# Issuing the pieces of turned attention weights, queries and keys from GpSimd, and taking each head norm's factor in one power

## The chip, the cores and the metric

The kernel runs on one core of one Trainium2 chip. The metric is the device time of one execution in microseconds (us). "PE" or TensorE multiplies matrices, "DVE" or VectorE and "ACT" or ScalarE work element by element, "POOL" or GpSimd does small element work and issues DMAs, and "SP" or SyncE issues DMAs only. A DMA issued by SP and one issued by GpSimd appear in the profile on different queues (q1 and q0).

## The reference, cut to what matters

The model is a trunk of two layers over 256 tokens of width 2048, with 256 memory tokens. Each layer has a token mixer of 12 heads of 128 beside 4 cross-attention heads into the memory, one output projection, and a squared-ReLU MLP of width 8192. Layer 0 has mixer A (neighbourhood attention), layer 1 has mixer B: grouped-query attention with 12 query heads and 4 key/value heads. Only mixer B normalises its heads:

```python
n = rms_norm(h, attn_norm[i])
z = n @ b_w_in[j]
q, k, v, qm = jnp.split(z, [MIX_WIDTH, MIX_WIDTH + KV_WIDTH, MIX_WIDTH + 2 * KV_WIDTH], axis=-1)
q = axial_rope(rms_norm(split_heads(q, N_MIX_HEADS), b_q_norm[j]))
k = axial_rope(rms_norm(split_heads(k, N_KV_HEADS), b_k_norm[j]))
...
def rms_norm(x, g):
    y = xf * lax.rsqrt(jnp.mean(xf * xf, axis=-1, keepdims=True) + EPS)
```

EPS is 1e-6. Every attention is softmax(q k^T) v in float32.

## The kernel before, in words

All weights are float32 and are loaded once, by SP, in chunks of 128 x 2048 (1 MB). Each half of a chunk is split by ScalarE and VectorE into a high and a low part (`hi`, `lo`, line 331 and the line before it), and TensorE makes each product as three: high by high, low by high, high by low. The chunks are worked off in halves called grains; a list of grains is the program's order, and a "tick" passes with each grain. A half is split three grains ahead of its products (`ahead=(8, 5, 3)`), a chunk's buffer is one of three (`raw`), and the split halves have four (`hi`, `lo`). Work that follows from a block of products (`later(n, ...)`) is put into the order n ticks on. The program is written in this order, and a planner that simulates a timeline places each engine's instructions in its own queue; an engine works its queue off in order.

Mixer A and the cross-attention of both layers, and most heads of mixer B, need the attention weights with keys along the partitions. They are not transposed by TensorE, but "turned": `attend` makes the scores and the softmax; `turned` lets VectorE transpose blocks of 32 x 32 within partitions (line 417), and `moved` carries the blocks between partitions by DMA: four "pieces" (line 382), one for each group of 32 partitions, go to a buffer in DRAM, 64 KB each, and one "return" (line 383), 256 KB, brings it back. The return is issued by GpSimd and waits for the pieces' landing. A few ticks later `attend2_turned` splits what came back into `pT`, and `attend3` makes the products `av` (lines 444 to 446). There are 26 such turns: 4 heads of cross-attention and 12 of mixer A in layer 0, 4 of cross-attention and 6 of mixer B in layer 1.

`heads_turned` does the same with a block of four heads of queries or keys in layer 1: two tiles of 128 tokens each, for the cross-attention queries (`b_qm_done`), the keys (`b_k_done`) and the first block of queries (`b_q_done`, block 0). Blocks 1 and 2 of the queries are transposed by TensorE (`heads_T`, tile `pt_h`). `turned_rows` uses `moved` as well, for the residual stream around the MLPs.

`normed_heads` takes a block of products in PSUM, unnormalised, and for each of two tiles: ScalarE squares each of four heads with the row's factor `rstd` as scale and sums the squares (line 1199); VectorE makes mean + EPS (`b_r_v`, line 337); GpSimd raises it to -0.5 (`b_r_r`, line 339) and multiplies by `rstd` (line 1202); ScalarE scales the heads by the result (line 1205); VectorE applies the rotary tables (lines 1207 to 1215), which gives `b_o`. It runs for the keys and for the three blocks of queries: 8 tiles.

Of the kernel before, what the change touches and what calls it, by code (L numbers as in the profile page):

```python
# [10 lines left out]
F32 = mybir.dt.float32  # L11
# [3 lines left out]
ALU = mybir.AluOpType  # L15
AX = mybir.AxisListType

P = 128
D = 2048
SEQ = 256  # L20
NT = SEQ // P
KT = D // P
DFF = 8192
HD = 128
# [7 lines left out]
EPS = 1e-6  # L32
# [59 lines left out]
def encoder_kernel(ctx: ExitStack, tc: tile.TileContext, t: dict, out: bass.AP):  # L92
    nc = tc.nc
# [3 lines left out]
    def opened(name, side="left", space=None, bufs=1):  # L97
        kw = {"space": space} if space else {}
        manager = tc.tile_pool(name=name, bufs=bufs, side=side, reuse_waits="tile", **kw)
        pools[name] = manager, manager.__enter__()  # L100
        return pools[name][1]

    def closed(*names):
        for name in names:
            pools.pop(name)[0].__exit__(None, None, None)

    const = opened("const")
    keep = opened("keep")
    small = opened("small", bufs=3)
# [10 lines left out]
    def open_ring():  # L120
        at.ring = opened("ring")
        at.cat = opened("cat")
# [32 lines left out]
    mhalf = const.tile([P, 8], F32, name="mhalf")  # L155
# [63 lines left out]
    def later(n, fn, *args):  # L219
        pending.append((state["tick"] + n, fn, args))  # L220
# [107 lines left out]
    def split(dst_hi, dst_lo, src):  # L328

        first = nc.scalar.activation(dst_hi, src, AF.Copy)  # L330
        return first, nc.vector.tensor_tensor(dst_lo, src, dst_hi.bitcast(F32), op=ALU.subtract)  # L331

    def rstd_of(ss, n, name):

        w = ss.shape[-1]
        v = small.tile([P, w], F32, tag="rs_v", name=f"{name}_v")
        nc.vector.tensor_scalar(v, ss, 1.0 / n, EPS, op0=ALU.mult, op1=ALU.add)
        r = small.tile([P, w], F32, tag="rs_r", name=f"{name}_r")
        nc.gpsimd.tensor_tensor(r, v, mhalf[:, :w], op=ALU.pow)
        return r  # L340
# [32 lines left out]
        return s  # L373


    def moved(dst, src):

        f = dst.shape[-1]
        x = dram.tile([P, 4, f], F32, tag=f"turn{f}", bufs=4, name="turn")
        to = x.rearrange("(b r) a f -> a r b f", r=32)  # L380
        for a in range(4):
            nc.sync.dma_start(to[a], src[32 * a : 32 * a + 32])
        nc.gpsimd.dma_start(dst, x)

    def scores(name):
        return at.work.tile([P, NT, SEQ], F32, tag="sc", bufs=at.scores, name=name)
# [27 lines left out]
    def turned(sc):  # L414

        x = scores("sc_t").rearrange("p a b -> p (a b)")
        nc.vector.transpose(x.rearrange("p (b k s j) -> p s k b j", b=4, k=2, s=2),
                            sc.rearrange("p s (k b r) -> p s k b r", k=2, b=4))
        back = sc.rearrange("p a b -> p (a b)").rearrange("p (a f) -> p a f", a=4)
        moved(back, x.rearrange("p (b f) -> p b f", b=4))  # L420
        return back

    def attend2_turned(back, o=0):
# [64 lines left out]
    def wide(name, at=0):  # L488
        room = keep.tile([P, KT * 512 + P], F32R, tag="wide", name=name)
        return room[:, at // 4 : at // 4 + KT * 512].rearrange("p (a b) -> p a b", b=512)  # L490
# [186 lines left out]
    def sum_squares(which, i, nb):  # L677
        sq = at.side.tile([P, 512], BF16, tag="junk", bufs=1, name="sq")
        nc.scalar.activation(sq, h[:, i, nb * 512 : (nb + 1) * 512], AF.Square,
                             accum_out=ssq[which][:, i, nb : nb + 1])  # L680

    def mean_square(which, n, name):

        s = small.tile([P, NT], F32, tag="ss0", name="ss_t")
        nc.vector.tensor_reduce(s, ssq[which][:, :, :n], axis=AX.X, op=ALU.add)
        v = keep.tile([P, NT], F32, tag=name, name=name)
        nc.vector.tensor_scalar(v, s, 1.0 / (n * 512), EPS, op0=ALU.mult, op1=ALU.add)
        return v

    def past(fn, ins=None):  # L690

        a, v = ins or box["ready"]
        with tc.issue_after(a.ins), tc.issue_after(v.ins):
            fn()

    def turned_rows(src, room, back):

        nc.vector.transpose(room.rearrange("p (b k i j) -> p i k b j", b=4, k=4, i=2),
                            src.rearrange("p i (k b r) -> p i k b r", k=4, b=4))
        back = back.rearrange("p (a f) -> p a f", a=4)  # L700
        moved(back, room.rearrange("p (b f) -> p b f", b=4))
        return back
# [259 lines left out]
    def add_scaled(hs, src, factor):  # L962
        nc.vector.scalar_tensor_tensor(hs, src, factor, hs, op0=ALU.mult, op1=ALU.add)
# [122 lines left out]
    def down_done(layer, nb):  # L1086
        def f(w):
            for i in range(NT):
                add_scaled(h[:, i, nb * 512 : (nb + 1) * 512], w.ps[i], box["inv"][:, i : i + 1])
            for i in range(NT):  # L1090
                sum_squares(2 * layer + 1, i, nb)
            if layer == 1:
                later(1, times_gf, nb)
                return
            if nb == 0:
                box["nT"] = wide("nT1", 480)
            if nb == 3:
                closed("mlp")
                open_ring()
            later(1, turned_input, nb)  # L1100
            if nb == 3:

                def norm():
                    box["rstd"] = keep.tile([P, NT], F32, name="rstd1")
                    box["mean"] = mean_square(1, 4, "mean")
                    nc.gpsimd.tensor_tensor(box["rstd"], box["mean"], mhalf[:, :NT], op=ALU.pow)
                later(2, norm)
        return f

# [63 lines left out]
    def heads_turned(src, dst):  # L1173

        backs = []
        for i in range(NT):
            room = scores("h_t").rearrange("p a b -> p (a b)")
            nc.vector.transpose(room.rearrange("p (b k j) -> p k b j", b=4, k=4),
                                src[i].rearrange("p (k b r) -> p k b r", k=4, b=4))
            back = src[i].rearrange("p (a f) -> p a f", a=4)  # L1180
            moved(back, room.rearrange("p (b f) -> p b f", b=4))
            backs.append(back)

        def heads_landed():
            for i in range(NT):
                hi, lo = (dst[:, :, x * SEQ + i * P : x * SEQ + (i + 1) * P].rearrange("p k (a j) -> p k a j", a=4)
                          for x in range(2))
                split(hi, lo, backs[i].rearrange("p a (k j) -> p k a j", k=4))

        later(5, lambda: past(heads_landed, box["splits"][-1]))  # L1190

    def normed_heads(w):
        cg, sg = box["rope"]
        outs = []
        for i in range(NT):
            y2 = at.work.tile([P, 4, HD], F32, tag="b_y2", name="b_y2")
            ss = small.tile([P, 4], F32, tag="b_ss", name="b_ss")
            for j in range(4):
                nc.scalar.activation(y2[:, j, :], w.ps[i][:, j * HD : (j + 1) * HD], AF.Square,
                                     scale=box["rstd"][:, i : i + 1], accum_out=ss[:, j : j + 1])  # L1200
            r = rstd_of(ss, HD, "b_r")
            nc.gpsimd.tensor_scalar(r, r, box["rstd"][:, i : i + 1], None, op0=ALU.mult)
            y = at.work.tile([P, 4, HD], F32, tag="b_y", name="b_y")
            for j in range(4):
                nc.scalar.activation(y[:, j, :], w.ps[i][:, j * HD : (j + 1) * HD], AF.Copy, scale=r[:, j : j + 1])
            o = at.work.tile([P, 4, HD], F32, tag="b_o", bufs=3, name="b_o")
            nc.vector.tensor_tensor(o, y, cg[:, i, None, :].to_broadcast([P, 4, HD]), op=ALU.mult)
            yv = y.rearrange("p h (a b c) -> p h a b c", a=2, b=2)
            y2v = y2.rearrange("p h (a b c) -> p h a b c", a=2, b=2)
            sv = sg[:, i, :].rearrange("p (a b c) -> p a b c", a=2, b=2)  # L1210
            for a in range(2):
                for b in range(2):
                    nc.vector.tensor_tensor(y2v[:, :, a, b, :], yv[:, :, a, 1 - b, :],
                                            sv[:, None, a, b, :].to_broadcast([P, 4, 32]), op=ALU.mult)
            nc.vector.tensor_tensor(o, o, y2, op=ALU.add)
            outs.append(o.rearrange("p a b -> p (a b)"))
        return outs

    def b_k_done(w):
        outs = normed_heads(w)  # L1220
        box["kT"] = keys("kT1")
        later(1, heads_turned, outs, box["kT"])
        later(3, rope_tables, "q", C_QN, SCALE)
# [190 lines left out]
```

## Time and profile before

| what | value |
|---|---|
| median of three runs | 2014.71 us (2011.62 to 2015.72) |
| the profiled execution | 2011.52 us |
| its span, first to last instruction | 2009.4 us |
| TensorE busy | 1997.4 us, 99% |
| VectorE busy | 1691.8 us, 84% |
| ScalarE busy | 1245.8 us, 62% |
| GpSimd busy | 142.7 us, 7% |
| DMA | 461.13 MB, mean 229 GB/s |

The stages lie so in the span: memory products from 0 to some 100 us, mixer A to some 330, output projection and MLP of layer 0 to some 1050, input products of mixer B to some 1220, its last heads beside the first products with w_o about 1220 to 1290, then the output projection and the MLP of layer 1 to the end. In the rows of time the first two columns are the start and the duration in us; the name before "<-" is the tile written, those behind it the tiles read; "L" is the line of the kernel; the bracket is the engine's idle time before the instruction and what ended it. "x4" merges four rows. In a view of one tile the three durations are least, median and greatest in ns, followed by the first and last start.

### The profile page before, as it was taken

The page shows a single profiled execution, that of the slowest core. Times are in us where ns is not written, and L with a number is a line of the kernel's source. Part 1 is how long each engine was busy: PE and PEld are TensorE (multiplying, and loading weights), DVE is VectorE, ACT ScalarE, POOL GpSimd, SP SyncE. Part 2 cuts the span into 40 slices and gives each one's busy share as a digit, 9 for nine tenths or more (in the row PEclk, how much of TensorE's full clock was granted, in tenths as well). Part 3 has the DMA queues.
Part 4 walks back from the last instruction along what each step waited for, and adds up shares of the span by engine and source line. Part 5 has one row for each costly group of instructions (what it writes and reads, how often), then busy time and mean ns, then how long its engine had stood idle before and what let it go on. Part 6 is the DMA issues. An engine that isn't in the chain of part 4 may idle for free.

```text
span 2009.4 us, 32896 instructions
## 1 busy us (share of the span) xinstructions
PE 1997.4 (99%) x12945; PEld 1807.2 (90%) x12945; DVE 1691.8 (84%) x2080; ACT 1245.8 (62%) x1650; POOL 142.7 (7%) x185
## 2 busy tenths in 40 slices
PE   9999999999999999999999999999999999999998
PEld 8999999899999999999988888889999999999997
DVE  6767767669998999999998778768989999999896
ACT  6755555557666666666655567657666666666664
POOL 0000000000000000000000112000000000000000
PEclk9999999999999999999999999999999999999999
DMA  7766666847777787787767776557777777777763
GB/s 286 300 224 217 219 222 210 329 134 236 223 232 232 233 233 235 217 244 236 216 215 262 257 260 213 216 190 239 227 231 223 235 229 234 225 239 231 235 224 115
DMA packets 121626, 461.13 MB, mean 229 GB/s; under 512 B 13824, under 2 KB 36992, under 8 KB 88320
## 3 DMA queue, kind: packets, MB, share of 16 engines
q1 hardware_dynamic: 100080, 412.90, 61.3%
q0 software_dynamic: 20816, 45.10, 10.5%
q8 instruction: 101, 1.65, 0.3%
q10 hardware_dynamic: 576, 1.05, 0.1%
q14 instruction: 53, 0.43, 0.1%
HBM read 411.80 MB, written 17.83 MB: 214 GB/s over the span
## 4 chain that ended last, share of the span: by engine, by line
PE 94%; DMA 2%; DVE 2%; issue 1%; ACT 1%; SPq 0%; POOLq 0%; POOL 0%; DVEq 0%; ACTq 0%
PE ps_u L825 12%; PE ps_u L824 12%; PE ps_u L823 12%; PE p L942 9%; PE p L941 9%; PE p L940 9%; PE ps_m L242 7%; PE ps_m L238 7%; PE ps_m L241 7%; PE ps_s L250 3%; PE ps_s L252 3%; PE ps_s L251 3%; DMA sc<-turn 1%; DVE lo L331 1%; DMA raw<-in_w_o 1%
## 5 line engine op out<-in xcount | busy, mean ns | idle before, releaser
L825 PE MATMUL ps_u<-hT,ul 128*128 128x256 f32 x2048 | 566.4, 277 | 0.0
L824 PE MATMUL ps_u<-hT,uh 128*128 128x256 f32 x2048 | 565.1, 276 | 0.0
L823 PE MATMUL ps_u<-hT,uh 128*128 128x256 f32 x2048 | 564.5, 276 | 0.0
L330 ACT ACTIVATE uh<-raw_U 128x1024 fp32r<-128x1024 f32 x278 | 294.5, 1061 | 297.8 <-PE ps_u L824 280.3
L824 PEld LDWEIGHTS ps_u<-hT,uh 128*128 128x128 f32 x2048 | 384.3, 188 | 6.6
L823 PEld LDWEIGHTS ps_u<-hT,uh 128*128 128x128 f32 x2048 | 384.2, 188 | 5.6
L825 PEld LDWEIGHTS ps_u<-hT,ul 128*128 128x128 f32 x2048 | 384.3, 188 | 0.1
L331 DVE TENSOR_TENSOR ul<-raw_U,uh 128x1024 fp32r<-128x1024 f32 x278 | 337.6, 1219 | 25.5 <-ACT uh L330 25.5
L331 DVE TENSOR_TENSOR lo<-raw,hi 128x1024 fp32r<-128x1024 f32 (+1 forms) x224 | 265.1, 1191 | 102.5 <-ACT hi L330 99.9
L330 ACT ACTIVATE hi<-raw 128x1024 fp32r<-128x1024 f32 (+1 forms) x224 | 230.4, 1038 | 166.3 <-PE ps_m L242 65.7
L330 ACT ACTIVATE th<-t 128x2048 fp32r<-128x2048 f32 x112 | 215.1, 1921 | 115.4 <-PE p L942 108.8
L331 DVE TENSOR_TENSOR tl<-t,th 128x2048 fp32r<-128x2048 f32 x112 | 256.2, 2288 | 28.1 <-ACT th L330 27.4
L331 DVE TENSOR_TENSOR bl<-b,bh 128x1536 fp32r<-128x1536 f32 x112 | 196.3, 1753 | 5.3 <-ACT bh L330 5.3
L330 ACT ACTIVATE bh<-b 128x1536 fp32r<-128x1536 f32 x112 | 166.7, 1488 | 19.4 <-PE p L942 13.2
L920 POOL DMA_DIRECT2D t<-b x112 | 96.5, 861 | 1126.0 <-DVE t L919 419.7
L942 PE MATMUL p<-th,a_s 128*128 128x512 f32 x448 | 176.3, 393 | 0.0
L941 PE MATMUL p<-tl,a_s 128*128 128x512 f32 x448 | 176.0, 393 | 0.0
L940 PE MATMUL p<-th,a_s 128*128 128x512 f32 x448 | 159.1, 390 | 0.0
L942 PE MATMUL p<-bh,a_s 128*128 128x512 f32 x336 | 131.7, 392 | 0.0
L941 PE MATMUL p<-bl,a_s 128*128 128x512 f32 x336 | 131.1, 390 | 0.0
L251 PE MATMUL ps_s<-nT,hi 128*128 128x256 f32 x448 | 124.1, 277 | 0.0
L250 PE MATMUL ps_s<-nT,hi 128*128 128x256 f32 x448 | 123.9, 277 | 0.0
(288 smaller groups left out, 3790.0 us busy)
## 6 DMA issues: line engine op xcount, KB each, us to landing
raw_U<-in_w_up SPq DMA_DIRECT2D x128, 1024.0 KB, 7.5
b<-in_w_pair SPq DMA_DIRECT2D x112, 768.0 KB, 4.9
raw<-in_w_o SPq DMA_DIRECT2D x32, 1024.0 KB, 5.6
t<-in_w_pair SPq DMA_DIRECT2D x112, 256.0 KB, 3.3
t<-b POOLq DMA_DIRECT2D x112, 256.0 KB, 7.3
raw<-in_w_b SPq DMA_DIRECT2D x21, 1024.0 KB, 5.9
raw<-in_w_av SPq DMA_DIRECT2D x12, 1024.0 KB, 5.1
raw<-in_w_aq SPq DMA_DIRECT2D x12, 1024.0 KB, 5.1
```

What stands on the lines that cost most here:

```text
L238: first = nc.tensor.matmul(w.ps[i], ah, hi[:, s], start=st, stop=False)
L241: nc.tensor.matmul(w.ps[i], ah, lo[:, s], start=False, stop=False)
L250: nc.tensor.matmul(ps, hi[:, s], acts[:, k, :SEQ], start=k == 0, stop=False)
L251: nc.tensor.matmul(ps, hi[:, s], acts[:, k, SEQ:], start=False, stop=False)
L330: first = nc.scalar.activation(dst_hi, src, AF.Copy)
L331: return first, nc.vector.tensor_tensor(dst_lo, src, dst_hi.bitcast(F32), op=ALU.subtract)
L823: nc.tensor.matmul(ps, hi[:, s], acts[:, k, :SEQ], start=k == 0, stop=False)
L824: nc.tensor.matmul(ps, hi[:, s], acts[:, k, SEQ:], start=False, stop=False)
L825: nc.tensor.matmul(ps, lo[:, s], acts[:, k, :SEQ], start=False, stop=k == KT - 1)
L940: nc.tensor.matmul(ps, a[:, 0, ai, :], hi[:, s], start=begins, stop=False)
L941: nc.tensor.matmul(ps, a[:, 0, ai, :], lo[:, s], start=False, stop=False)
L942: nc.tensor.matmul(ps, a[:, 1, ai, :], hi[:, s], start=False, stop=ends)
```

## The change

`moved` gets a parameter for the queue of the four pieces, SP by default. `turned` and `heads_turned` pass GpSimd; `turned_rows` does not. So the pieces of the 26 turns and of the six tiles of `heads_turned`, 128 DMAs, are issued by GpSimd, in the same queue as their returns and the powers.

In `normed_heads` the squares are taken of the unscaled products. With s for the row's `rstd` and m for the row's `mean` (1 / s^2), the factor s * (s^2 * q + EPS)^-0.5 is the same as (q + EPS * m)^-0.5, where q is the mean of the unscaled squares. `least` = EPS * `mean` is made once, two columns; VectorE's instruction takes it in place of the constant EPS, and GpSimd's multiplication by `rstd` is gone.

```diff
-    def moved(dst, src):
+    def moved(dst, src, queue=nc.sync):
...
         for a in range(4):
-            nc.sync.dma_start(to[a], src[32 * a : 32 * a + 32])
+            queue.dma_start(to[a], src[32 * a : 32 * a + 32])
         nc.gpsimd.dma_start(dst, x)
...
-        moved(back, x.rearrange("p (b f) -> p b f", b=4))
+        moved(back, x.rearrange("p (b f) -> p b f", b=4), nc.gpsimd)
...
                     nc.gpsimd.tensor_tensor(box["rstd"], box["mean"], mhalf[:, :NT], op=ALU.pow)
+                    box["least"] = keep.tile([P, NT], F32, name="least")
+                    nc.vector.tensor_scalar(box["least"], box["mean"], EPS, None, op0=ALU.mult)
...
-            moved(back, room.rearrange("p (b f) -> p b f", b=4))
+            moved(back, room.rearrange("p (b f) -> p b f", b=4), nc.gpsimd)
...
                 nc.scalar.activation(y2[:, j, :], w.ps[i][:, j * HD : (j + 1) * HD], AF.Square,
-                                     scale=box["rstd"][:, i : i + 1], accum_out=ss[:, j : j + 1])
-            r = rstd_of(ss, HD, "b_r")
-            nc.gpsimd.tensor_scalar(r, r, box["rstd"][:, i : i + 1], None, op0=ALU.mult)
+                                     accum_out=ss[:, j : j + 1])
+            v = small.tile([P, 4], F32, tag="rs_v", name="b_r_v")
+            nc.vector.tensor_scalar(v, ss, 1.0 / HD, box["least"][:, i : i + 1], op0=ALU.mult, op1=ALU.add)
+            r = small.tile([P, 4], F32, tag="rs_r", name="b_r_r")
+            nc.gpsimd.tensor_tensor(r, v, mhalf[:, :4], op=ALU.pow)
```

## The prediction

> **What bounds the kernel now.** I read the page's busy times and its chain first, then TensorE's own waits, then TensorE's rows of time in the one stretch where its rhythm breaks.
>
> ```profile
> span 2009.4 us, 32896 instructions
> PE 1997.4 (99%) x12945; PEld 1807.2 (90%) x12945; DVE 1691.8 (84%) x2080; ACT 1245.8 (62%) x1650; POOL 142.7 (7%) x185
> PE 94%; DMA 2%; DVE 2%; issue 1%; ACT 1%; SPq 0%; POOLq 0%; POOL 0%; DVEq 0%; ACTq 0%
> ...
> PE pt_h L1169 <- DVE b_o L1215: 0.3, 1, 0.3
> PE ps_m L241 <- DVE lo L331: 0.2, 1, 0.2
> ```
>
> TensorE is busy 1997.4 of 2009.4 us, and it carries 94% of the chain. The two last lines are the only waits of TensorE that lie in the part that the change touches. So a gain can come only from pauses of TensorE, and a loss only from new ones. A busy share hides short pauses (ends of matmuls are modelled), so I look at the starts, where mixer B's last queries meet the first products with w_o:
>
> ```profile
> 1247.35 0.40 PE L241 MATMUL ps_m<-lo,cat 128*128 128x512 f32 x1
> 1247.59 0.62 PE L238 MATMUL ps_m<-hi,cat 128*128 128x512 f32 x2
> 1248.50 0.87 PE L1169 MATMUL pt_h<-ident,b_o 128*128 128x128 f32 x6 [0.29 <-DVE b_o L1215]
> 1249.13 0.48 PE L242 MATMUL ps_m<-hi,cat 128*128 128x512 f32 x1
> 1249.83 0.50 PE L241 MATMUL ps_m<-lo,cat 128*128 128x512 f32 x1 [0.22 <-DVE lo L331]
> ...
> 1255.58 0.39 PE L241 MATMUL ps_m<-lo,cat 128*128 128x512 f32 x1
> 1256.07 0.73 PE L242 MATMUL ps_m<-hi,cat 128*128 128x512 f32 x2
> ...
> 1257.34 0.39 PE L241 MATMUL ps_m<-lo,cat 128*128 128x512 f32 x1
> 1257.72 0.39 PE L444 MATMUL av<-pT,vb 128*128 128x256 f32 x1
> ```
>
> A 512-column product is followed by the next start 0.23 us later (1247.35 to 1247.59 is such a step). Two products from 1247.59 should be followed at 1248.05; the next start is 1248.50: 0.45 us lost, for b_o. From 1249.13 the next is due at 1249.36 and comes at 1249.83: 0.47 lost, for a weight half. From 1255.58: due 1255.81, came 1256.07, 0.26 lost. From 1257.34: due 1257.57, came 1257.72, 0.15 lost. Together 1.33 us in 2009.4: that is all that I find to be won here in the profiled execution, and it is a third of the 0.2% (4.0 us) that a measurement of this kernel can tell from no change.
>
> **The change, part by part.** Moved are the pieces of `turned` (26 turns of attention weights, four pieces each: 104) and of `heads_turned` (three calls, two tiles each, four pieces: 24), 128 DMAs of 64 KB. The pieces of `turned_rows` stay on SP. Each turn is four pieces to DRAM and one return by GpSimd, which waits for the pieces' landing.
>
> ```profile
> L382 SPq DMA_DIRECT2D turn<-sc_t x104: 302/432/1397, 113.9 to 1247.6; - x104
> DMA to landing us min/median/max: 1.6/2.8/5.9
> 129.79 1.84 SPq L382 DMA_DIRECT2D turn<-sc_t  x4
> L383 POOL DMA_DIRECT2D sc<-turn x26: 538/548/744, 119.2 to 1250.3; - x26
> DMA to landing us min/median/max: 2.9/4.0/7.0
> 1227.21 1.23 POOL L383 DMA_DIRECT2D sc<-turn  x2 [16.92 <-DMA turn<-sc_t]
> L551 POOL DMA_DIRECT2D cat<-mem_v x2: 729/730/732, 1090.2 to 1090.9; - x2
> ```
>
> The first landing row is of SP's 64 KB pieces, the second of GpSimd's 256 KB returns. SP issues four pieces in 1.84 us, so the last, itself 0.43 long, starts 1.4 us after the first. GpSimd issues two returns in 1.23 us, 0.62 each; four pieces start over 1.9 us: 0.5 us later. The trace has no such piece from GpSimd; between the two landing minima lie 1.3 us, part of which is the return's fourfold bytes. I take 0.5 of it, because a small piece is nearer to SP's row in size and to GpSimd's only in its path. So a turn comes back L = 1.0 us later. The upper end is spacing as in the row of 0.73 (0.8 us), all 1.3 us of landing and a return that stands behind one piece of another turn (0.6): 2.7 us. The lower end is below zero: SP's pieces land in 2.8 us at the median against 1.6 at best, because some stand behind a weight load on the same queue; off that queue up to 1.2 us could go, less the 0.5 for issue: -0.7. I keep both ends for the range.
>
> GpSimd's load: 128 x 0.62 = 79 us on 142.7, still under 12% of the span, so no engine becomes full.
>
> What is L worth? The consumer is the split `pT` on ScalarE and VectorE, then the three `av` products. The rows below are of the five turns of mixer A with least room: VectorE's half of the split and the first product that reads it.
>
> ```profile
> L445 PE MATMUL av<-pT,vm x2: 280/282/283, 142.4 to 142.8; 128*128 128x256 f32 x2
> L331 DVE TENSOR_TENSOR pT<-sc,pT x1: 693/693/693, 140.8 to 140.8; 128x512 fp32r<-128x512 f32 x1
> ...
> L445 PE MATMUL av<-pT,va x2: 276/276/276, 265.0 to 265.3; 128*128 128x256 f32 x2
> L331 DVE TENSOR_TENSOR pT<-sc,pT x1: 693/693/693, 263.4 to 263.4; 128x512 fp32r<-128x512 f32 x1
> ...
> L445 PE MATMUL av<-pT,vl x2: 281/282/282, 290.5 to 290.8; 128*128 128x256 f32 x2
> L331 DVE TENSOR_TENSOR pT<-sc,pT x1: 694/694/694, 289.1 to 289.1; 128x512 fp32r<-128x512 f32 x1
> ...
> L445 PE MATMUL av<-pT,vm x2: 281/282/282, 147.8 to 148.2; 128*128 128x256 f32 x2
> L331 DVE TENSOR_TENSOR pT<-sc,pT x1: 693/693/693, 145.3 to 145.3; 128x512 fp32r<-128x512 f32 x1
> ...
> L445 PE MATMUL av<-pT,va x2: 276/276/276, 194.0 to 194.3; 128*128 128x256 f32 x2
> L331 DVE TENSOR_TENSOR pT<-sc,pT x1: 693/693/693, 191.5 to 191.5; 128x512 fp32r<-128x512 f32 x1
> ```
>
> Room is the product's start less the split's end: 142.4 - 141.5 = 0.9; 265.0 - 264.1 = 0.9; 290.5 - 289.8 = 0.7; 147.8 - 146.0 = 1.8; 194.0 - 192.2 = 1.8. The other turns have 2.1 us or more. Each head's lateness counts anew, since each chain starts from its own scores on TensorE. At L = 1.0 the pauses are 0.1 + 0.1 + 0.3 = 0.5 us. That is the one cost that I find: +0.5.
>
> ScalarE waits for landings too, and weight halves stand behind its wait. Their cover is the code's distance: a half is split three grains before its products, and a grain is twelve products of 0.23 us, so some 8 us; 1 us more takes none of it away. If it were used up, the halves after each turn would be late next.
>
> **Off SP.** Behind the pieces on SP stand the weight loads. In the stretch above:
>
> ```profile
> 1245.39 1.19 DVE L331 TENSOR_TENSOR lo<-raw,hi 128x1024 fp32r<-128x1024 f32 x1
> 1245.86 2.21 SPq L382 DMA_DIRECT2D turn<-sc_t  x3
> 1248.16 0.44 SPq L186 DMA_DIRECT2D raw<-in_w_o  x1
> 1253.50 1.06 ACT L330 ACTIVATE hi<-raw 128x1024 fp32r<-128x1024 f32 x1 [2.38 <-DMA raw<-in_w_o]
> ```
>
> A split frees a weight buffer at 1246.58, but SP is among the pieces until 1248.07, and the load goes out at 1248.16; ScalarE then waits 2.38 us for it. With the pieces gone the load can go 1.5 us earlier. The pauses of 0.26 and 0.15 follow from that split; I count them as won: -0.4. The 0.47 pause is not the load's: VectorE was late with a half whose data it had. Elsewhere weight loads wait for a buffer, not for pieces, and nothing is won.
>
> **The norm.** Per tile of queries or keys the old chain is a VectorE row, a power and a multiplication on GpSimd; the new one is a VectorE row with a pointer in place of the constant, and the power.
>
> ```profile
> L339 POOL TENSOR_TENSOR b_r_r<-b_r_v,mhalf x8: 1001/1037/1412, 1133.9 to 1236.1; 128x4 f32<-128x4 f32 x8
> L1202 POOL TENSOR_SCALAR b_r_r<-b_r_r,rstd x8: 304/924/1746, 1136.0 to 1237.2; 128x4 f32<-128x4 f32 x8
> 1234.16 1.41 POOL L339 TENSOR_TENSOR b_r_r<-b_r_v,mhalf 128x4 f32<-128x4 f32 x1 [1.85 <-DVE b_r_v L337]
> ```
>
> Eight multiplications go, 0.3 to 1.7 us each, 0.9 in the middle. One VectorE instruction of two columns is added (`least`), long before it is read; the squares' pointer scale goes, on ScalarE, whose count of instructions stays. The last pair of tiles is the only one near TensorE's pauses (b_o, 0.45 us). But the same queue now takes the pieces: a turn is transposed at about the time that the power starts at 1234.16, and four pieces ahead of a power cost it 2.5 us. Bounds for b_o: 1.2 us earlier (both multiplications gone, no piece ahead), or 1.6 us later (2.5 - 0.9). The order on GpSimd isn't known, and the middle is near zero: I take 0 and leave the 0.45 us pause where it is.
>
> **Sum.** +0.5 - 0.4 + 0 = +0.1 us on the profiled execution, 2011.52 us with a span of 2009.4. The median of the runs shown is 2014.71, their extremes 2011.62 and 2015.72. With the profiled one these are four executions with a mean of 2013.4, so the median of three may stand somewhat high; I forecast 2014.0, about halfway between mean and median.
>
> **Rivals.** A, slower: turns come back much later than 1 us, and `av` waits in mixer A. It decides from L = 2.2: pauses 1.3 + 1.3 + 1.5 + 0.4 + 0.4 = 4.9, less 0.4, is +4.5 us: 2018.5. At the bound of 2.7 the five give 8.2 with 1.8 + 1.8 + 2.0 + 0.9 + 0.9 = 7.4 and some 0.8 of the turns with 2.1 to 2.4 us of room: about 2021.8. For it: the landing rows of GpSimd. Against it: between L = 1.0 and 2.2 lies nearly all that the rows differ by. Chance 0.11.
>
> A', the same place with another cause: GpSimd's issue is held up by VectorE, which is 84% busy. If each piece waited for one weight half (1.19 us, the row above), four pieces would add 4.8 us, L would be 5.8, and the five turns alone would give 4.9 + 4.9 + 5.1 + 4.0 + 4.0 = 22.9, less 0.4: 2036.5. Against it: the 26 issues of GpSimd beside the same VectorE took 538 to 744 ns, median 548. Chance 0.02. The Trainium skill has this as a rule: its page "SBUF — State Buffer", section "SBUF: two separate sides", says that while VectorE runs an instruction in a two-port mode GpSimd is locked out and cannot write the descriptors of its DMAs. The 26 rows do not agree with it for the instructions that VectorE runs here.
>
> B, slower: on GpSimd the power stands behind a return that waits for its pieces. At 1234 that is 2.5 us of issue and 2.9 of landing before the power, 5.4 against 0.9 saved: b_o 4.5 us later, and the pause before pt_h grows by as much: 2018.5. Against it: the work before has powers placed between returns. Chance 0.06.
>
> C, faster by over 0.2%: the 3.2 us between the median run and the profiled one lie in late loads behind pieces, and go with them, and all 1.33 us of pauses too: 2014.7 - 3.2 - 1.3 = 2010.2. Chance 0.16.
>
> D, the likeliest, within 0.2%: 0.65. Its own range is 2010.7 to 2018.0 (0.2% either side of the median would be 2010.7 to 2018.7).
>
> So faster 0.16, same 0.65, slower 0.11 + 0.02 + 0.06 = 0.19. The range for 8 in 10 reaches to C's 2010.2 and just past the points where A and B decide: 2010.0 to 2019.0.
>
> **What would show it.** Right: SP's L382 keeps 40 pieces, GpSimd has 128 more DMA rows of 0.5 to 0.7 us; the pieces' first issue to the return's issue grows from some 4 to 5 us; `av` L444 or L445 shows starts late by a few tenths near the three tight turns; the load of w_o near 1248 goes out as soon as its buffer is free. Wrong: pieces that take over 0.8 us each, TensorE waits for `pT` or `pt_h` of several us, or a power that waits behind a return.

## The result, and the profile after

The changed kernel takes 2045.74 us (median of 5 runs, 2045.13 to 2048.13) against 2014.53 (2011.62 to 2015.72): a ratio of 1.016, 95% interval 1.0146 to 1.0175. Forecast were 2014.0 us, a range of 2010.0 to 2019.0 and, as the likeliest, a time within 0.2% of the kernel before; no rival reached beyond 2036.5. Executions far slower than the others of their kernel are left out of the ratios (of e9 below it was the profiled one, with 7190.89 us, so that e13 runs the same kernel again). The page of the profiled execution after, busy times and the largest groups (line, engine, tiles, shapes, count, busy us and mean ns):

```profile
span 2043.6 us, 32822 instructions
PE 2030.0 (99%) x12945; PEld 1839.6 (90%) x12945; DVE 1699.7 (83%) x2081; ACT 1243.8 (61%) x1650; POOL 206.6 (10%) x305
...
L825 PE MATMUL ps_u<-hT,ul 128*128 128x256 f32 x2048 | 575.0, 281 | 0.0
L824 PE MATMUL ps_u<-hT,uh 128*128 128x256 f32 x2048 | 574.8, 281 | 0.0
L823 PE MATMUL ps_u<-hT,uh 128*128 128x256 f32 x2048 | 574.6, 281 | 0.0
```

The span grew by 34.2 us and TensorE's busy time by 32.6, with the same 12945 products. So TensorE hardly waits more: its products themselves take longer, and most of the loss lies in a stage that the change doesn't touch. `ps_u` is the MLP's up projection. In the stage that the change does touch, TensorE's waits are no more than these two (us in total, times, longest):

```profile
PE ps_m L242 <- DVE cat L331: 1.3, 1, 1.3
PE ps_m L238 <- ACT cat L330: 0.4, 1, 0.4
```

Where the 34 us lie is read from TensorE's busy time on one tile, stretch by stretch (stretch in us, its length, busy us and count). First the tile `ps_u` before, then after:

```profile
483.00:1070.00 587.00, 309.32 (x2630) 1.00 0.76 229
1330.00:2050.00 720.00, 359.73 (x3065) 1.00 0.68 206
sum 2050.00, PE 721.76; mean PE 144.35
```

```profile
483.00:1070.00 587.00, 325.46 (x2664) 1.00 0.75 225
1330.00:2050.00 720.00, 374.66 (x3072) 0.99 0.70 214
sum 2050.00, PE 747.44; mean PE 149.49
```

That is 25.7 us more for the 6144 up products, and in both layers, at a granted clock of 0.99 to 1.00. The same sum for `ps_s` (the input products of 256 columns) goes from 204.91 to 210.76, for `ps_m` (products of 512 columns in the mixers) from 515.40 to 521.01, for `p` (the down products) from 561.65 to 557.91. Together 25.7 + 5.9 + 5.6 - 3.7 = 33.5 of 34.2 us. The starts show what a product lost. Rows of time before, then after:

```profile
600.00 0.28 PE L823 MATMUL ps_u<-hT,uh 128*128 128x256 f32 x1
...
601.02 0.28 PE L823 MATMUL ps_u<-hT,uh 128*128 128x256 f32 x1
```

```profile
600.09 0.28 PE L823 MATMUL ps_u<-hT,uh 128*128 128x256 f32 x1
...
601.15 0.28 PE L823 MATMUL ps_u<-hT,uh 128*128 128x256 f32 x1
```

Nine steps from one product to the next lie between the two starts of each fence: 1.02 us before, 113 ns each; 1.06 us after, 118 ns each. In both traces nearly all starts of `ps_u` come 113 or 118 ns behind the last, and hardly any between. Before, `ps_u` is at 113 nearly throughout. After, it is at 113 in the first up grains and goes to 118 at 483.8 us, just behind the first down products, and stays there.

What could do this in a stage whose instructions are the same? The new tile `least` holds 8 bytes per partition, but takes a slot of 32. In the built programs every tile allocated behind it lies 32 bytes higher: `small`, the ring with `raw`, `hi` and `lo`, `cat`, and all of the MLP's tiles (`a_s`, `bh`, `bl`, `th`, `tl` from 64 to 96 past a multiple of 256). `hT`, `nT`, `uh` and `ul` stay. From here on a place is a tile's address modulo 256 bytes.

### The profile page after: what moved, and what is told of

Same layout as the page of the kernel before. It is cut to its first block, busy times and chain, and to the rows that moved or that the text cites. A ratio compares the mean times of both kernels' runs of the same rounds, so it can differ in the third digit from the quotient of the medians.

```text
span 2043.6 us, 32822 instructions
## 1 busy us (share of the span) xinstructions
PE 2030.0 (99%) x12945; PEld 1839.6 (90%) x12945; DVE 1699.7 (83%) x2081; ACT 1243.8 (61%) x1650; POOL 206.6 (10%) x305
## 4 chain that ended last, share of the span: by engine, by line
PE 97%; DMA 1%; DVE 1%; ACT 0%; issue 0%; SPq 0%; POOL 0%; POOLq 0%; DVEq 0%; ACTq 0%
PE ps_u L824 12%; PE ps_u L825 12%; PE ps_u L823 12%; PE p L940 9%; PE p L942 9%; PE p L941 9%; PE ps_m L242 8%; PE ps_m L241 8%; PE ps_m L238 8%; PE ps_s L252 3%; PE ps_s L251 3%; PE ps_s L250 3%; DMA raw<-in_w_km 1%; PE av L445 0%; PE av L444 0%; PE av L446 0%
## 5 line engine op out<-in xcount | busy, mean ns | idle before, releaser
L825 PE MATMUL ps_u<-hT,ul 128*128 128x256 f32 x2048 | 575.0, 281 | 0.0
L824 PE MATMUL ps_u<-hT,uh 128*128 128x256 f32 x2048 | 574.8, 281 | 0.0
L823 PE MATMUL ps_u<-hT,uh 128*128 128x256 f32 x2048 | 574.6, 281 | 0.0
L823 PEld LDWEIGHTS ps_u<-hT,uh 128*128 128x128 f32 x2048 | 391.7, 191 | 5.5
L824 PEld LDWEIGHTS ps_u<-hT,uh 128*128 128x128 f32 x2048 | 385.1, 188 | 6.1
L251 PE MATMUL ps_s<-nT,hi 128*128 128x256 f32 x448 | 125.9, 281 | 0.0
L252 PE MATMUL ps_s<-nT,lo 128*128 128x256 f32 x448 | 125.7, 281 | 0.0
```

The source lines that it names most:

```text
L251: nc.tensor.matmul(ps, hi[:, s], acts[:, k, SEQ:], start=False, stop=False)
L252: nc.tensor.matmul(ps, lo[:, s], acts[:, k, :SEQ], start=False, stop=k == KT - 1)
L823: nc.tensor.matmul(ps, hi[:, s], acts[:, k, :SEQ], start=k == 0, stop=False)
L824: nc.tensor.matmul(ps, hi[:, s], acts[:, k, SEQ:], start=False, stop=False)
L825: nc.tensor.matmul(ps, lo[:, s], acts[:, k, :SEQ], start=False, stop=k == KT - 1)
```

## The experiments

A kernel's ratio is to the kernel before, run on the same chip beside it.

**e1, the tile alone.** The kernel before, with the two lines that make `least`, which nothing reads.

```diff
+                    box["least"] = keep.tile([P, NT], F32, name="least")
+                    nc.vector.tensor_scalar(box["least"], box["mean"], EPS, None, op0=ALU.mult)
```

> The kernel before with only the new tile of 8 bytes (`least`, and the VectorE instruction that fills it; nothing reads it). Pieces stay on SP, the norm stays as it was. The tile takes 32 bytes of each partition below the small, ring, cat and MLP tiles and moves them all up by 32 bytes. Theory P (placement: TensorE's 256-column products take 118 ns instead of 113 where tiles lie 32 bytes higher): about 2043 us, with the products of u at a mean of 118 ns. Rival Q (the pieces on GpSimd are the cause): 2014.5 us, within 3. Rival O (the planner's other order on TensorE is the cause): anything, and not tied to the tile.

Measured 2044.86 us, ratio 1.0156 (1.0136 to 1.0176). Its sum for `ps_u` is that of the changed kernel:

```profile
sum 2050.00, PE 747.29; mean PE 149.46
```

**e2, all of the change but the tile.** `least` is put into two unused columns of the tile `mhalf`, so that nothing moves.

```diff
-                    box["least"] = keep.tile([P, NT], F32, name="least")
+                    box["least"] = mhalf[:, 4 : 4 + NT]
```

> The whole change (pieces on GpSimd, one power), but `least` lies in columns 4 and 5 of the constant tile `mhalf`, which are free, so that no other tile moves. Theory P: all but a few us of the loss is gone, 2012 to 2018 us, u products at 113 ns. Rival Q: 2045 us as with the change.

Measured 2013.0 us, ratio 0.9997 (0.9987 to 1.0007); the sum for `ps_u`:

```profile
sum 2050.00, PE 721.89; mean PE 144.38
```

So the whole 1.6% is the tile's place, and what the change is about comes to nothing within 0.13%. Rival O falls too: in the traces the products of e1 stand in the order of the kernel before, those of e2 in the order of the changed kernel, and the times are the other way round.

**e3 and e4, which of the moved tiles.** e3 is the kernel before with the MLP's tiles 32 bytes up (`MLP_AT` sets their offset), with the same products in the same order. e4 has the tile of e1, but the MLP's tiles back in place, so only `small`, the ring and `cat` are moved.

```diff
-MLP_AT = 192
+MLP_AT = 224
```

> The kernel before with the gap at the bottom of the MLP's tiles widened by 32 bytes (MLP_AT 224 for 192): every instruction on every engine is the same and in the same order, and only z, c, a, bh, bl, th, tl lie 32 bytes higher. Theory P: the MLP's share of the loss, u products +25.5 us, the down products -4.1, the last products +1.2: about +22 us, 2037 us. Rival Q and rival O (order): 2014.5 us.

> As the run with the tile only, with the MLP's gap narrowed by 32 bytes, so that the MLP's tiles lie where they lay before and only the small, ring and cat tiles are 32 bytes higher. Theory P: the attention stages' share, some +6 us for the S products and +4 for the M products: 2022 to 2026 us, u products at 113 ns. Rival Q: 2014.5 us.

e3: 2032.38 us, 1.0097 (1.0071 to 1.0122). e4: 2023.68 us, 1.0051 (1.0032 to 1.0071). Both count, and they nearly add: 18.1 + 9.4 = 27.5 of e1's 30.6 us. The sums say where: `ps_u` in e3, then `ps_s` in e4:

```profile
sum 2050.00, PE 745.61; mean PE 186.40
```

```profile
sum 2050.00, PE 212.27; mean PE 53.07
```

In e3 `ps_u` has 23.9 us more, although neither of its operands moved; in e4 it is `ps_s`, which has 7.4 more, and `ps_m` (519.47, 4.1 more), of whose operands many did move against each other (the ring moved, `nT` did not).

**e5 and e6, one operand of the down products alone.** An unused tile of 32 bytes between `a_s` (stationary) and the moving halves parts them: in e5 the moving halves go up, in e6 `a_s` goes down.

```diff
+            if part == 0 and n == 0:
+                at.mlp.tile([P, 8], F32, tag="gap2", name="gap2")
```

> The kernel before, with an unused tile of 32 bytes set between the tiles of the MLP: the stationary halves a_s of the down projection stay where the kernel before has them (64 bytes past a multiple of 256), its moving halves bh, bl, th and tl go up by 32 bytes. The planner's order of the instructions changes with it. Theory M (the place of the moving operand of the products that run just ahead sets the cadence in which the up projection's products follow each other, 113 or 118 ns): most of the 6144 up products at 118 ns, so about 2014 + 18 = 2032 us, as when the whole set of tiles moved. Rival S (the place of the stationary operand a_s does it): 113 ns, 2012 to 2017 us.

> The counterpart: the stationary halves a_s (with c and z) go down by 32 bytes, the moving halves bh, bl, th and tl stay where the kernel before has them. Theory M: 113 ns in the up products, 2012 to 2017 us. Rival S: 118 ns, about 2032 us. A third possibility is that only the distance of the two counts (both kernels with the 32 bytes between them slow, about 2032 us each).

e5: 2024.02 us, 1.0048 (1.0028 to 1.0067). e6: 2024.18 us, 1.0053 (1.003 to 1.0075). TensorE's order is that of the kernel before in both. Neither theory expected that, and both fall; the third possibility (only the distance counts) had the two alike, but at 2032. `ps_u` stays at 724.1 in both: it is the down products themselves that lost, 569.43 (e5) and 570.77 (e6) against 561.65. So the distance between two operands counts, by another rule than what slows `ps_u`.

**e7 and e8, the MLP's tiles 64 and 128 bytes up** (`MLP_AT` 256 and 320), order unchanged.

> The kernel before with all tiles of the MLP 64 bytes higher, the same instructions in the same order on every engine. If the cadence goes with a place modulo 64 bytes: 113 ns, 2012 to 2017 us. If any move away from the places of the kernel before makes it slow: 2030 to 2035 us.

> The same with all tiles of the MLP 128 bytes higher. Period of 64 or 128 bytes: 2012 to 2017 us. Period of 256 bytes, or any move slow: 2030 to 2035 us.

e7: 2022.19 us, 1.0048 (1.0034 to 1.0062), `ps_u` 727.26, mostly at 113 ns. e8: 2035.63 us, 1.0113 (1.0084 to 1.0142), `ps_u` 742.82, mostly at 118. So the pace of `ps_u` has no period of 64 or 128 bytes, and not every move puts it at 118, though e7 is slower too (by 9.2 us; `ps_u` has 5.5 more in its profiled execution): the rule had to be measured by itself.

**m1, the places by themselves.** A kernel of its own with TensorE alone.

```python
for k in range(n):   # n = 24; m, s: places of the moving and the stationary operand
    nc.tensor.matmul(ps[:, :size], (sh, sh, sl)[k % 3][:, s // 4 + j * P : s // 4 + (j + 1) * P],
                     (mh, ml, mh)[k % 3][:, m // 4 + c * 512 : m // 4 + c * 512 + size], ...)
```

> A kernel of its own, in which no other engine and no DMA works beside TensorE: grains of 24 products each (three products to a pair of chunks, the stationary chunk changed as in the kernel), with the moving and the stationary operand at every pair of the eight places 0, 32, ... 224 past a multiple of 256 bytes: once 64 grains of 512 columns, twice 64 grains of 256 columns in two orders, and 64 times a grain of 512 columns at each pair with a grain of 256 columns behind it that stands at the up projection's own places (moving 160, stationary 224). The encoder is left out: the output is x. Theory P (the pair of places alone sets the pace): a pair's median start to start is 113 or 118 ns for 256 columns (226 or 232 ns for 512), the same for a pair in both orders, and the 64 grains behind are all alike. Rival H (the pace is handed on from the grain ahead): the same pair comes out at 113 in one order and 118 in the other in many of the 64, and the grains behind at the same places are split between the two according to the pair ahead. Rival T (it needs the traffic of the other engines or of DMA): one pace, within 1 ns, everywhere.

Median start to start, worked out from the trace's starts, by the distance (stationary less moving place, modulo 256); in each entry eight pairs, in each of two orders:

```
distance         0        32       64       96       128       160      192       224
512 columns, ns  227      232-235  231-235  234-235  229-237   231-232  229-233   233-234
256 columns, ns  120      117-118  113/118  117-119  118-120   118-121  113/118   116-119
```

(One grain of 512 at distance 128, the first of the kernel, ran at 426 ns throughout and is left out.) Theory T falls: nothing else runs, and the pace still depends on the places. Both other theories are right in part. The distance sets which pace is possible: 512 columns go at 227 ns only at distance 0, and 256 columns reach 113 only at 64, and twice in 16 grains at 192. At distance 64 the 256-column pace has two values, and 2 of the 8 pairs there (and 2 of 8 at 192) came out at 113 in one order and at 118 in the other; of the other pairs six differ by 2 or 3 ns. Of the 64 grains of 256 columns that stood at the same places behind a grain of 512, 40 ran at 113 and 24 at 118. Either that is handed on or it is chance; m2 repeats the case.

Now the code reads differently. `nT` lies at 128 and the ring's `hi` at 128, or at 192 where it is stationary: distance 0 for the products of 512 columns and 64 for those of 256. `hT` lies at 160 and `uh` at 224: 64. `a_s` and the moving down halves lie at 64: 0. `least` turned the ring's 0 and 64 into 224 and 96; by the table that is 227 to 233-234 and 113 to 117-119 ns. The traces agree: after, products of `hi` with `nT` start 234 ns apart at the median (227 before) and those of `nT` with `hi` 118 (113 before), while those of `hi` with `cat`, which moved together, stay at 227.

**m2, the MLP's cycle by itself.** TensorE alone: 12 and 9 down products at one place c, then 48 up products at the up projection's own places, three cycles for each c, in two orders of the c.

```python
for c in turns:
    for _ in range(3):
        grain("th", 512, c, c, 12); grain("bh", 512, c, c, 9); grain("up", 256, 160, 224, 48)
```

> TensorE alone again, in the MLP's own cycle: 12 products of 512 columns (as with th and tl), 9 of 512 (bh and bl), 48 of 256 columns at moving 160 and stationary 224 (as in the up projection), three cycles for each place c of both operands of the down products (0, 32, ... 224), the places in two orders. The encoder is left out: the output is x. Theory H (the pace is handed on, and the place of the down products decides which): a second and third cycle repeat each other, c = 64 (the kernel before) gives 113 ns in the 48 and c = 96 (the changed kernel) 118, as they did in the encoder; from the single grains before, 0, 128 and 192 give 113 and 32, 160 and 224 give 118. Rival T (the traffic of other engines picks the pace): no such link between c and the pace, or cycles of one c that differ.

Rows of time at c = 64 (the kernel before), then at c = 96 (the changed kernel):

```profile
175.09 0.28 PE L50 MATMUL up<-mh,sh 128*128 128x256 f32 x1
...
178.49 0.28 PE L50 MATMUL up<-mh,sh 128*128 128x256 f32 x1
```

```profile
454.43 0.28 PE L50 MATMUL up<-mh,sh 128*128 128x256 f32 x1
...
456.56 0.28 PE L50 MATMUL up<-mh,sh 128*128 128x256 f32 x1
```

30 products in 3.40 us are 113 ns each; 18 in 2.13 us are 118. All six cycles of a c agree: 0, 64 and 128 give 113; 32, 96, 160, 192 and 224 give 118. That is e3 (96) and e8 (192) mostly at 118, and e7 (128) and the kernel before (64) mostly at 113. The expectation had 192 among the places that give 113; the grain of m1 behind 192 and 192 had run at 118, so that was misread, and m2 agrees with all eight grains of m1 behind equal places. Even the small gain of `p` is there: behind 113 the 12 products of `th` settle at 230 to 231 ns for c = 64, behind 118 at 227 for c = 96; in the encoder the medians are 229 (`th`) and 231 (`tl`) before and 227 for both in e3. Rival T falls here too.

**e11 and e12, the old distances at new places.** If that is the rule, the tile can stay. e11 is e1, and e12 the whole change, with `nT` and the halves that meet it moved up with the ring, and the MLP moved back.

```diff
-MOVING_AT = 160
+MOVING_AT = 192
...
-MLP_AT = 192
+MLP_AT = 160
...
-            box["nT"] = wide("nT0", 480)
+            box["nT"] = wide("nT0", 512)
...
-                box["nT"] = wide("nT1", 480)
+                box["nT"] = wide("nT1", 512)
```

> The kernel before with the unused tile least (2044.9 us) and the tiles set so that every pair of operands has its old distance again: the MLP's tiles 32 bytes down (where they were), nT and the moving halves that meet it 32 bytes up, with the ring, which least has moved. Same instructions in the same order on every engine as the 2044.9 us run. Theory D (the distance of the operands modulo 256 bytes and the pace handed on set the cost, not where the tiles lie): 2012 to 2016 us. Rival A (the absolute places of the ring, cat or nT matter): 2020 us or more, as with the ring alone 32 bytes up (2023.7).

> The whole change with its tile least, and the same three places set. Theory D: 2011 to 2017 us, as the change without the tile (2013.0). Rival A: 2020 us or more. Neither theory expects it below 2010.

e11: 2015.88 us, 1.0015 (1.0005 to 1.0024), with TensorE's products in the order of e1 (2044.86). e12: 2016.28 us, 1.0017 (1.0007 to 1.0026), against 2045.74 for the change as it was made. Theory D holds for all but a small part: e11 is 2.5 us and e12 2.9 us over the kernel before that ran beside them, where e1 was 30.6 over its own. These 2.5 to 2.9 us are not explained: in e11 `ps_u` has 723.86 and `ps_s` 207.70, 2.1 and 2.8 over the kernel before.

**e9, e10 and e13, the two parts of the change alone**, with no tile moved: e9 issues the pieces from GpSimd and keeps the old norm; e10 has the new norm with `least` in `mhalf` and the pieces on SP; e13 is e9 again.

> One part of the change alone: the 128 pieces are issued by GpSimd, the norm is that of the kernel before, no tile is added and none moves. By the prediction's terms (0.5 us through the five tightest av turns, less 0.4 us of SP's relief): 2014.6 us against 2014.5, range 2012 to 2018. With rival A of the prediction (returns 2.2 us later or more): 2018.

> The other part alone: unscaled squares and one power, with least in two columns of a tile that exists, so that none moves; the pieces stay with SP. By the prediction's term of 0.0 us: 2012 to 2016 us. With rival B of the prediction (the power behind the returns) there is no effect here, since the returns stay with SP: also 2012 to 2016; a time above 2018 would say that the norm costs by itself.

> The queue's part alone once more, for a trace of an execution at the usual pace. If the 8 us of the first measurement are waits of TensorE (rival A of the prediction: returns 2.2 us late or more): pauses ahead of av products or of the first products on landed rows that sum to 5 us or more, the products at their old pace. If they are the pace: products of 256 columns at 118 ns or of 512 at 232 in some stage that a changed order of the attention's products leads into, with pauses of 1 to 2 us in all. Time 2018 to 2022 us in both; 2012 to 2016 would say that the first measurement was disturbed.

e9: four executions of 2019.05 to 2021.82 us, 1.0041 (1.0027 to 1.0054). e10: 2015.54 us, 1.0012 (0.9999 to 1.0026): no change that can be told by the median, but its eleven executions lie in two groups, six from 2009.87 to 2015.54 and five from 2018.47 to 2019.48. The profiled one (2018.69) is of the second: TensorE waits 3.7 us before an `av` at 1238.47, and behind it the granted clock is 0.50 for 6.8 us. e13: 2021.02 us, 1.0036 (1.0021 to 1.0051), so the queue's part alone is slower, by some 8 us (7.6 by the medians of e13). The waits of TensorE in e13, the rows around the longer one, and GpSimd's rows there:

```profile
PE av L444 <- ACT pT L330: 3.3, 1, 3.3
PE ps_m L238 <- ACT b_y L1205: 3.1, 1, 3.1
```

```profile
1256.17 0.63 PE L242 MATMUL ps_m<-hi,cat 128*128 128x512 f32 x2
1260.08 0.38 PE L444 MATMUL av<-pT,vb 128*128 128x256 f32 x1 [3.28 <-ACT pT L330]
```

```profile
1243.59 2.22 POOL L382 DMA_DIRECT2D turn<-sc_t  x4 [1.23 <-DVE sc_t L417]
1245.80 1.10 POOL L383 DMA_DIRECT2D sc<-turn  x2
1250.17 2.25 POOL L382 DMA_DIRECT2D turn<-sc_t  x4 [3.27 <-DVE sc_t L417]
1252.41 0.56 POOL L383 DMA_DIRECT2D sc<-turn  x1
```

TensorE stands still from 1256.80 to 1260.08, and GpSimd's rows say why. By their order the return at 1252.41 belongs to the four pieces that were out by 1245.81, the last of which had landed by 1247.3. It stands behind the pieces of the next turn, and these wait for their transposition on VectorE: GpSimd idles 3.27 us and then issues for 2.25 before the return may go. It takes 5.2 us to land, so it is there at 1257.6; then ScalarE has a softmax and a weight half ahead of `pT`. That is rival A (turns that come back too late), by a return behind the pieces of another turn, and in mixer B's last heads instead of mixer A. With the pieces on SP no return could stand behind them. The other pause, of 3.1 us from 1236.39, ends when ScalarE has scaled the last queries (`b_y`). GpSimd had their factor ready at 1236.23, but ScalarE began to scale at 1238.29, behind a weight half and a softmax, so most of this pause is ScalarE's order; the powers, in turn, began at 1232.54, 2.3 us after VectorE's first `b_r_v` was there, behind four pieces. With the new norm too (e2) the planner puts these last products in another order, the two pauses are 0.4 and 1.25 us, and 8 us of loss are gone. So the two parts do not add: their sum misses the whole by some 8 us even if e10 counts as nothing. The order that the planner finds differs in all three kernels; that a shorter norm chain is what lets it find the better one was not tested.

**e14 and e15, a place that might beat both.** m2 has one place with neither slower pace: c = 0 gave 227 ns in `th` and 113 in `up`.

```diff
-PLAIN_AT = 96
+PLAIN_AT = 32
...
-MLP_AT = 192
+MLP_AT = 128
```

> The kernel before with the MLP's tiles at 0 past a multiple of 256 bytes (they lie at 64) and the up halves of the plain grains moved with them, so that every distance of operands is the old one; same instructions in the same order. Theory H (the pace is handed on by a rule of places that TensorE alone shows): the 1344 products of th and tl at 227 ns instead of 230, the 6144 of the up projection at 113 as before, so about 206.0 + 103.2 us become 204.0 + 101.9 as they were at place 96, 3.3 us less: 2010 us against 2013.4, ratio 0.9984. Rival A (the pace in the encoder needs other traffic, or only the tuned place 64 holds the 113): up products at 118 in part or all, 2015 to 2035.

> The change without its tile, with the same place 0 for the MLP. Theory H: 3.3 us under the change without its tile (2013.0): 2010 us, faster than both kernels, ratio to the kernel before 0.998. Rival A: 2015 to 2035.

e14: 2011.82 us, 0.9998 (0.9988 to 1.0009). e15: 2013.15 us, 1.0004 (0.9995 to 1.0012). The 113 ns hold, so rival A falls, but the gain isn't there: `p` has 559.91 us in e14, 1.7 less than before instead of 3.3, and `ps_u` 723.69, 1.9 more. No version of these runs beats the kernel before by more than can be told.

## Why the prediction was wrong

**The step that failed** is one sentence in its part on the norm: "One VectorE instruction of two columns is added (`least`), long before it is read". It cost the instruction, rightly, at nothing. It did not cost the tile that the instruction writes. That tile is worth +30.6 us alone (e1), and no rival had it. What the runs showed in place of the zero is a slower pace of unchanged products: `ps_u` at 118 ns instead of 113 (25.7 us), the rest in `ps_s` and `ps_m`. The range ended at 2019.0 because it was built of waits only: "a loss only from new ones" (pauses) was the false premise, since a product's own pace is not fixed. The diff and the code had the hint: the constants `MOVING_AT`, `MLP_AT` and `STILL_AT` set where tiles lie modulo 256 bytes and nothing else.

**The pieces on GpSimd.** The mechanism and its size were near. Forecast were 0.62 us for a piece and 79 us more for GpSimd; after, the rows of the pieces, and the landings of pieces and returns:

```profile
L382 POOL DMA_DIRECT2D turn<-sc_t x104: 551/551/750, 115.1 to 1265.3; - x104
L382 POOL DMA_DIRECT2D turn<-h_t x24: 551/552/609, 1147.6 to 1216.9; - x24
```

```profile
turn<-sc_t POOLq DMA_DIRECT2D x104, 64.0 KB, 3.3
sc<-turn POOLq DMA_DIRECT2D x26, 256.0 KB, 4.6
```

128 x 0.551 = 70.5 us, less eight multiplications (0.9 us each in the middle), is about the 63.9 us by which GpSimd's busy time grew. Pieces land in 3.3 us at the median (2.8 before) and returns in 4.6 (4.0 before), and four pieces take 0.4 us more to issue: L is some 1.5 us, not 1.0, within the forecast -0.7 to 2.7. The term that was mis-sized is the return behind another turn: the prediction allowed 0.6 us for one piece in front of it, and it was four pieces and the wait for their transposition, 5.1 us from the landing of its own pieces to its issue (e13). What all this costs came out as forecast in the sum (e2, 2013.0 us) by luck, since the parts were wrong. The five tight `av` turns of mixer A show no wait after; TensorE's order is another one there. The order is not given, as the sum assumed; it is made anew for each kernel. The cost came in mixer B's last heads instead: none to speak of with the new norm (e2), 8 us without it (e13). That is more than the 4.5 us of rival A, and in a place that the prediction did not name.

**Rival A'** (VectorE holds up GpSimd's issue) did not come: 128 pieces beside a VectorE that is 83% busy have a median of 551 ns and a longest of 750. The lock-out in the Trainium skill's page "SBUF — State Buffer", section "SBUF: two separate sides", is not seen in these rows either; whether VectorE ran an instruction in a two-port mode meanwhile, no run here shows.

**Off SP and the norm.** The pauses at 1247 to 1257 (1.33 us) went elsewhere rather than away: after, there are waits of 0.4 and 1.3 us, 0.53 and 1.43 by the starts, so the 0.4 us that the prediction counted as won is not seen. The norm alone is 1.0012 with an interval that includes no change (e10), but five of its eleven executions are some 3 us and more above the others, and the one of them that was profiled has a pause of 3.7 us and a slower clock behind it, which the forecast of 0 did not name.

## What to carry to other kernels

Where TensorE is 99% busy, an edit that allocates anything is an edit to the addresses behind it: list which tiles move and whether two operands of a hot product, or of one that runs just ahead of it (e3), change their distance or place, and put a small new value into a tile that exists. When a kernel gets slower without waits, compare the products' start-to-start times stage by stage with the kernel before; a slower pace at an unchanged granted clock, in a stage that was not edited, points to placement. To tell an edit's merit from its side effect, run it once without moving a tile.

## What was not expected of the hardware

The pace of a product depends on where its operands lie against each other modulo 256 bytes (227 against 229 to 237 ns for 512 columns, 113 against 116 to 121 for 256), and at distance 64 it has two values and keeps the one that the products ahead hand on (113 or 118 ns: 24 to 26 us over the 6144 up products). This shows with TensorE alone. The Trainium skill's page "TensorE: Matmul & The Clock Gate", section "Step-by-step: what each phase is for", says that loading the next weights does not take read bandwidth from the running matmul, since TensorE has two read ports of its own. In m1 the pace goes with the distance between the two operands, which that sentence does not lead one to expect; what in the hardware does it, these runs do not show.

A pause of TensorE can cost more than its length. In e13, from some 1.2 us after the pause that ended at 1239.47, products of 512 columns come 0.43 us apart instead of 0.23 for some 3 us (rows of time). The granted clock is 0.50 in that stretch and in one behind the other pause, 1.00 around them (the column behind the count in the last two rows: stretch, length, busy us and count, clock, share and rate of DMA):

```profile
1239.47 0.50 PE L238 MATMUL ps_m<-hi,cat 128*128 128x512 f32 x1 [3.08 <-ACT b_y L1205]
...
1241.24 0.63 PE L238 MATMUL ps_m<-hi,cat 128*128 128x512 f32 x1
1241.67 0.63 PE L241 MATMUL ps_m<-lo,cat 128*128 128x512 f32 x1
```

```profile
1240.60:1244.00 3.40, 3.40 (x10) 0.50 0.95 367
1261.10:1264.50 3.40, 3.40 (x17) 0.50 0.00 0
```

At half the clock 3.4 us do the work of 1.7, so each of the two pauses costs an estimated 1.7 us more: 3.25 + 3.45 (by the starts) + 3.4, less the 1.3 of pauses that the kernel before has there, is 8.8 us, as much as its span (2018.2) exceeds that before (2009.4). The same page, section "What's actually happening", says that after an idle window of about 3.4 us the array falls to half its clock. The factor agrees; the length does not quite, since in e2 and e15 the clock fell to 0.50 for 3.4 us behind pauses of 0.5 and 1.4 us, while behind the same two pauses in the changed kernel and in e12 it stayed at 1.00.
